# Block sums of the up projection's weights, added in DRAM during latent attention, with another order of its seven products and another loading of the latents' weights

## The chip, the cores and the metric

The kernel runs on one NeuronCore of a Trainium2 chip. The metric is device time in microseconds (us), as a median over executions. Engines: TensorE (PE) multiplies, VectorE (DVE), ScalarE (ACT) and GpSimd (POOL) work on elements, SyncE (SP) issues DMA transfers; POOL can issue them too.

## The reference

One encoder layer over two requests of 2048 and 256 tokens (D_MODEL 1024, eight heads of latent attention, eight of neighbourhood attention, D_FF 2816):

```python
h = rms_norm(x, g_mix_pre)
z = h @ w_in                                   # latents, rope key, nq, nk, nv
a = mla_attention(c_q, c_kv, k_rope, g_q_lat, w_q_up, g_kv_lat, w_kv_up)
n = neighborhood_attention(nq, nk, nv, na_rpb)
mix = jnp.concatenate([a, n], axis=-1) @ w_o
x = x + rms_norm(mix, g_mix_post)
h = rms_norm(x, g_ffn_pre)
x = x + rms_norm(conv_ffn(h, w_ffn_up, ffn_conv_w, ffn_conv_b, w_ffn_down), g_ffn_post)

def conv_ffn(x, w_up, conv_w, conv_b, w_down):
    h = x @ w_up                               # 1024 x 5632
    hp = jnp.pad(h, ((0, 0), (pad, pad), (0, 0)))
    hc = conv_b
    for t in range(CONV_W):                    # width 3, over positions
        hc = hc + hp[:, t:t + S] * conv_w[t]
    g, u = jnp.split(hc, 2, axis=-1)
    return (jax.nn.gelu(g, approximate=True) * u) @ w_down
```

All values are float32.

## The kernel before, in words

**Precision.** Each factor of a product is split into a high part (`split`: ACT copies it, L95) and a low part (DVE subtracts, L96), and three matmuls (`mm3`, L120 to L122) make one product.

**Order of work.** A tile scheduler puts the instructions of each engine in one order, which the engine then keeps; each DMA queue starts its transfers in the order in which its engine issues them. The stages: input projection (to some 280 us), neighbourhood attention (to some 700), preparation and loop of latent attention (794 to 1653), output projection in 18 tiles of 128 tokens (to some 1925), up projection (to some 2960), down projection.

**Neighbourhood attention** runs `n` = 144 iterations of half a unit, each with scores, softmax and transposes (`turn`: probabilities `pb` L404, their transposes `pT` L411, copies `pth`, `ptl`) and values. Between them `queries_rest` (in the first half) makes the remaining query and key projections, and `latents` (from iteration `mid + LATE` = 78) the latents' projection, a quarter of a token tile per call. At `mid` = 72 the latents' weights take the place of the weights `w2` of the first half: eight blocks are loaded through `qk_hl`, a pool of two buffers which also carries queries and keys to DRAM, and split into `w3h` and `w3l`.

**Latent attention** is a loop of 528 steps of 128 keys by 512 queries: scores `pS`, exponentials `ph` (ACT, L623, six buffers), low parts `pl` (DVE), a running sum `acc` (POOL, L634), and values some steps behind. `later` is a table from a step to what is done there.

**Up projection.** The product of weights (blocks W00, W01, W10, W11: gate or value rows by halves of D_MODEL) and inputs is made by seven products of block sums for each of three parts of the tokens (L1051) and 22 hidden tiles, 66 units. `PLAN` is the list of products; a product is 12 matmuls of 386 columns. Each needs a factor of weights (`w_factor`: a raw block or a block sum, 128x512, then split into `wh`, `wl`) and one of inputs (`x_factor`, once for each part, `xh`, `xl`; sums made by `x_source`, L1152). The results lie in PSUM in one of eight banks `pz`, two products add onto the bank of an earlier one (`onto`), and `s`, `v`, `t`, `hg`, `hu` are combinations of them (L1194 is the helper's line, on DVE or POOL); `conv` is the convolution (L1222 on ACT, L1225 on DVE), and POOL multiplies gate by value (L1241).

**Block sums of weights.** Five sums for each of 22 hidden tiles go to `ws_d` in DRAM. Those of hidden tiles 0 to 5 are made in the output projection (`weight_sums`, loads L138, additions on POOL L149, stores L144). Those of 6 to 21 are made in part 0 of the up projection (`w_source`: five additions on POOL, L1132, and five stores per hidden tile). Parts 1 and 2 load all of them from `ws_d`.

## Time and profile before

| | |
|---|---|
| median of three runs | 3509.68 us (3509.68, 3509.68, 3519.23) |
| the profiled execution | 3507.15 us, its span 3505.4 us |
| mean granted clock of TensorE | 0.989 |
| PE busy | 3368.9 us (96%) |
| DVE busy | 2385.9 us (68%) |
| ACT busy | 1837.8 us (52%) |
| POOL busy | 1376.2 us (39%) |

The span goes from the first to the last instruction of the profiled execution; its own time is some 2 us longer. A busy share is an average over stages that differ. The granted clock is TensorE's clock as a share of full speed, which is 2.4 GHz.

### The profile page before, as it was taken

How to read it: one execution, taken by the hardware profiler on the slowest of the kernel's cores; microseconds unless marked ns; L12 is line 12 of the kernel's file. 1: busy time of each engine (PE TensorE's matmuls, PEld its weight loads, DVE VectorE, ACT ScalarE, POOL GpSimd, SP SyncE). 2: the span in 40 equal slices, each digit the busy share in tenths (PEclk: the TensorE clock that was granted, in tenths of full speed). 3: DMA queues.
4: the chain of work that ended last, by engine and by line, in shares of the span. 5: the costliest groups of instructions: out<-in, count | busy, mean ns of one | idle time of the engine just before them, and what ended most of it. 6: DMA issues, size and time to landing. Idle time of an engine off the chain costs nothing.

```text
span 3505.4 us, 51290 instructions
## 1 busy us (share of the span) xinstructions
PE 3368.9 (96%) x17806; PEld 2913.6 (83%) x17806; DVE 2385.9 (68%) x3774; ACT 1837.8 (52%) x3463; POOL 1376.2 (39%) x1216
## 2 busy tenths in 40 slices
PE   8999989989999999999989999899999999999999
PEld 7889979967777777766778999899989999888887
DVE  5325555588988888898345999987789776224332
ACT  4225556567777777777234544555555554223121
POOL 0022323157777778775521477632232222000110
PEclk9999999999999999999999999999999999999999
DMA  8789889341000000011995655465546555434553
GB/s 269 253 258 231 213 191 237 122 149 26 13 15 14 16 14 13 18 47 48 267 256 150 195 170 172 144 192 149 149 113 194 151 150 179 149 117 134 187 186 125
DMA packets 338068, 497.24 MB, mean 142 GB/s; under 512 B 69584, under 2 KB 213072, under 8 KB 330832
## 3 DMA queue, kind: packets, MB, share of 16 engines
q1 hardware_dynamic: 302576, 417.87, 39.7%
q0 software_dynamic: 35232, 76.10, 8.6%
q8 instruction: 140, 2.29, 0.3%
q14 instruction: 120, 0.98, 0.1%
HBM read 337.90 MB, written 155.37 MB: 141 GB/s over the span
## 4 chain that ended last, share of the span: by engine, by line
PE 74%; DVE 10%; ACT 6%; DMA 5%; issue 3%; POOL 2%; SPq 1%; ACTq 0%; POOLq 0%; DVEq 0%
PE pz L1291 21%; PE po L122 6%; PE po L120 6%; PE po L121 6%; PE po L646 3%; PE pS L619 3%; PE pg L600 3%; PE pl L647 3%; PE pS L621 3%; PE pS L620 3%; PE pO L448 2%; DVE wl L96 2%; PE pT L120 2%; PE pT L411 2%; PE pT L122 1%
## 5 line engine op out<-in xcount | busy, mean ns | idle before, releaser
L1291 PE MATMUL pz<-xh,wh 128*128 128x386 f32 (+1 forms) x1848 | 633.3, 343 | 20.8 <-DVE hg L1194 11.5
L1291 PE MATMUL pz<-xl,wh 128*128 128x386 f32 (+1 forms) x1848 | 630.2, 341 | 6.1 <-DVE xl L96 5.7
L1291 PE MATMUL pz<-xh,wl 128*128 128x386 f32 (+1 forms) x1848 | 628.8, 341 | 6.0 <-DVE wl L96 6.0
L634 POOL TENSOR_TENSOR acc<-acc,ph 128x512 f32<-128x512 f32 x434 | 568.3, 1309 | 103.8 <-ACT ph L623 82.3
L96 DVE TENSOR_TENSOR wl<-raw,wh 128x512 fp32r<-128x512 f32 (+1 forms) x470 | 444.0, 953 | 36.2 <-ACT wh L95 36.0
L95 ACT CAST wh<-raw 128x512 fp32r<-128x512 f32 (+1 forms) x470 | 288.9, 627 | 235.4 <-PE pz L1291 221.3
L623 ACT ACTIVATE ph<-pS 128x512 fp32r<-128x512 f32 (+1 forms) x528 | 312.4, 592 | 183.5 <-PE pS L621 98.6
L626 DVE TENSOR_TENSOR pl<-pS,ph 128x512 fp32r<-128x512 f32 (+1 forms) x528 | 354.6, 673 | 71.9 <-ACT pS L624 68.3
L110 POOL TENSOR_TENSOR rs_r<-rs_m,mhalf 128x1 f32<-128x1 f32 (+1 forms) x90 | 74.3, 826 | 800.4 <-DVE rs_m L107 800.1
L1291 PEld LDWEIGHTS pz<-xh,wh 128*128 128x128 f32 x1848 | 350.5, 190 | 31.3 <-DVE hg L1194 16.6
L1291 PEld LDWEIGHTS pz<-xl,wh 128*128 128x128 f32 x1848 | 351.1, 190 | 8.1 <-DVE xl L96 7.3
L1291 PEld LDWEIGHTS pz<-xh,wl 128*128 128x128 f32 x1848 | 350.7, 190 | 7.5 <-DVE wl L96 7.4
L602 DVE TENSOR_REDUCE mx<-pg 128x1 f32<-128x512 f32 (+1 forms) x528 | 343.0, 671 | 12.6 <-PE pg L600 10.1
L1241 POOL TENSOR_TENSOR cg<-cg,cu 128x768 f32<-128x768 f32 (+1 forms) x66 | 165.2, 2503 | 445.3 <-DVE cu L1225 324.6
L122 PE MATMUL po<-dh,xr 128*128 128x512 f32 x792 | 311.7, 394 | 0.4 <-DVE xr L96 0.4
L121 PE MATMUL po<-dl,xr 128*128 128x512 f32 x792 | 311.8, 394 | 0.0
L120 PE MATMUL po<-dh,xr 128*128 128x512 f32 x792 | 311.6, 393 | 0.0
L624 ACT ACTIVATE pS<-pS 128x512 f32<-128x512 f32 (+1 forms) x528 | 311.5, 590 | 0.0
L96 DVE TENSOR_TENSOR xr<-xt,xr 128x1408 fp32r<-128x1408 f32 x37 | 60.6, 1639 | 330.8 <-ACT xr L95 330.8
L95 ACT CAST xr<-xt 128x1408 fp32r<-128x1408 f32 x37 | 50.7, 1369 | 382.1 <-PE po L121 368.3
L619 PE MATMUL pS<-ql,kbh 96*128 96x512 f32 (+1 forms) x528 | 215.2, 408 | 5.0 <-DVE pl L626 2.9
L621 PE MATMUL pS<-qh,kbh 97*128 97x512 f32 (+1 forms) x528 | 211.8, 401 | 0.1
(259 smaller groups left out, 7923.6 us busy)
## 6 DMA issues: line engine op xcount, KB each, us to landing
raw<-ws_d SPq DMA_DIRECT2D x250, 256.0 KB, 2.7
raw<-in_w_ffn_up_dram SPq DMA_DIRECT2D x164, 256.0 KB, 3.2
xt<-g_d SPq DMA_DIRECT2D x37, 704.0 KB, 4.4
graw<-g_d SPq DMA_DIRECT2D x35, 704.0 KB, 5.1
g_d<-cg SPq DMA_DIRECT2D x110, 192.0 KB, 2.3
ws_d<-raw SPq DMA_DIRECT2D x80, 256.0 KB, 2.0
xl<-xs_d POOLq DMA_DIRECT2D x18, 1024.0 KB, 8.8
xh<-xs_d POOLq DMA_DIRECT2D x18, 1024.0 KB, 7.1
```

Of the source, the lines that this page charges most:

```text
L95: self.nc.scalar.copy(out=hi, in_=src)
L96: self.nc.vector.tensor_tensor(out=lo, in0=src, in1=hi.bitcast(F32), op=ALU.subtract)
L120: mm(out=out, lhsT=lh, rhs=rh, start=start, stop=False)
L121: mm(out=out, lhsT=lh, rhs=rl, start=False, stop=False)
L122: mm(out=out, lhsT=ll, rhs=rh, start=False, stop=stop)
L602: nc.vector.tensor_reduce(out=u.mx[:, i, c:c + 1], in_=pg[:, :n], axis=AX.X, op=ALU.max)
L619: mm(out=pS[:, :nq], lhsT=u.kh[0:QKD, kc], rhs=u.ql[:, :nq], start=True, stop=False)
L621: mm(out=pS[:, :nq], lhsT=u.kh[:, kc], rhs=u.qh[:, :nq], start=False, stop=True)
L623: nc.scalar.activation(out=ph[:, :nq], in_=pS[:, :nq], func=AF.Exp, scale=scale)
L626: nc.vector.tensor_tensor(out=pl[:, :nq], in0=pS[:, :nq], in1=ph[:, :nq].bitcast(F32), op=ALU.subtract)
L634: eng.tensor_tensor(out=u.acc[:, :nq], in1=ph[:, :nq].bitcast(F32), op=ALU.add, in0=u.p0[:, :nq].bitcast(F32) if j == 1 else u.acc[:, :nq])
L1291: nc.tensor.matmul(out=pz[:, :w], lhsT=l[:, kk, :], rhs=r[:, kk, :w], start=onto is None and kk == 0 and e == 0, stop=kk == 3 and e == 2, ...
```

## The change

1. All block sums are made in DRAM, by transfers that POOL issues in the loop of latent attention: four sums instead of five, each in two halves of 11 hidden tiles (2.88 MB a transfer). Eight transfers copy a first block to `ws_d` (from step 20 on, one in eight steps), eight more add a second block or another sum to it (four from step 160, two from 270, two from 360). `weight_sums` in the output projection and `w_source` are gone.
2. The seven products use other sums and another order, (1, 5, 3, 7, 2, 6, 4); one product (4) adds onto another (7) instead of two. `value` comes before `gate`; one combination per unit moves from DVE to POOL (`hu`), another falls away.
3. The latents' weights come block by block: block k is loaded at iteration `mid - 12 + k` into a pool of its own, and split two iterations later into a slot of `w2`, which is now eight tiles. `latents` starts at `mid`.

```diff
-    def weight_sums(self, raw_buf, out_buf, todo):
...
+        block = lambda rc, js: a["w_ffn_up"].rearrange("(r j) p k c -> r j p (k c)", r=2)[
+            rc[0], js, :, 512 * rc[1]:512 * rc[1] + 512]
+        first, stages = [], [[], [], []]
+        def late(**k):
+            self.tc.keep_in_program_order(nc.gpsimd.dma_start(**k))
+        for i, (m, (b0, b1)) in enumerate(self.WSUM.items()):
+            for js in (slice(0, 11), slice(11, NFF)):
+                first.append(lambda i=i, b0=b0, js=js: late(out=self.ws_d[js, i], in_=block(b0, js)))
+                src = self.ws_d[js, list(self.WSUM).index(b1)] if isinstance(b1, int) else block(b1, js)
+                stages[max(0, i - 1)].append(lambda i=i, src=src, js=js: late(
+                    out=self.ws_d[js, i], in_=src, accum_op=ALU.add, max_dma_last_dim=2048))
+        return [first] + stages
...
+            w2 = [[w2p.tile([P, KD, P], F32R, name=f"w{2 * f + i}") for i in range(2)] for f in range(4)]
...
+            def load_lat(k):
+                raw = lwp.tile([P, LAT], F32, name="raw")
+                nc.sync.dma_start(out=raw, in_=a["w_in"][k * P:(k + 1) * P, 0:LAT])
+                def convert():
+                    wlat[k] = w2p.tile([P, 2, LAT], F32R, name=f"w{k}")
+                    self.split(raw, wlat[k][:, 0, :], wlat[k][:, 1, :])
+                return convert
...
+                if 0 <= i - (mid - 10) < KD:
+                    lat_w[i - (mid - 10)]()
+                if 0 <= i - (mid - 12) < KD:
+                    lat_w[i - (mid - 12)] = load_lat(i - (mid - 12))
+                if i == mid - 4:
+                    Rest.blocks = {0: fetch(0)}
                 if i == mid:
-                    wlat = [w[:, :, :LAT] for w in w_tiles(w2p, 3, 512)]
-                    Rest.n, Rest.blocks = 0, {0: fetch(0)}
-                    load_w(lambda: st.tile([P, 2, NB], F32, name="qk_hl").rearrange("p a b -> p (a b)"), wlat, 0, LAT)
-                if i >= mid + LATE and Rest.n < 4 * NT:
+                    Rest.n = 0
+                if i >= mid and Rest.n < 4 * NT:
                     latents()
...
+            for q, part in enumerate(self.weight_sums()):
+                for r, f in enumerate(part):
+                    later.setdefault((20, 160, 270, 360)[q] + 8 * r, []).append(f)
...
-            if t < 7:
-                sums()
-                sums()
-            if t == 7:
-                flush()
...
-    ORDER = (1, 5, 3, 4, 2, 7, 6)
-    WSUM = {1: ((0, 0), (1, 1), 1), 2: ((1, 0), (1, 1), 1), 5: ((0, 0), (0, 1), 1), 6: ((1, 0), (0, 0), -1),
-            7: ((0, 1), (1, 1), -1)}
-    WRAW = {3: (0, 0), 4: (1, 1)}
+    WSUM = {4: ((0, 1), (1, 1)), 5: ((0, 0), (0, 1)), 1: ((0, 0), 4), 2: ((1, 0), 1)}
+    WRAW = {3: (0, 0), 6: (1, 0), 7: (1, 1)}
...
-    PLAN = [(k, m) for k in range(3 * NFF) for m in (1, 5, 3, 4, 2, 7, 6)]
-    PLAN[4:9] = [(1, 1), (1, 5), (0, 2), (0, 7), (0, 6)]
-    NRAW = 13
+    PLAN = [(k, m) for k in range(3 * NFF) for m in (1, 5, 3, 7, 2, 6, 4)]
+    PLAN[4:9] = [(1, 1), (1, 5), (0, 2), (0, 6), (0, 4)]
+    NRAW = 10
...
-    def w_source(self, i):
...
+        def value(u):
+            tt(nc.vector, u.hu[:, 1, :u.w], u.b[6][:, :u.w], u.t[:, :u.w], 1)
+            u.cu = conv(u.hu, NFF + u.j, u.n, "u")
         def gate(u):
-            tt(nc.vector, u.hg[:, 0, :u.w], u.b[1][:, :u.w], u.v[:, :u.w], 1)
+            tt(nc.vector, u.hg[:, 0, :u.w], u.v[:, :u.w], u.b[7][:, :u.w], -1)
             u.cg = conv(u.hg, u.j, u.n, "g")
             nc.scalar.activation(out=u.cg[:, :, :u.n], in_=u.cg[:, :, :u.n], func=AF.Gelu_apprx_tanh)
+            nc.gpsimd.tensor_tensor(out=u.cg[:, :, :u.n], in0=u.cg[:, :, :u.n], in1=u.cu[:, :, :u.n], op=ALU.mult)
...
-            onto = {7: 1, 6: 3}.get(m)
+            onto = {4: 7}.get(m)
...
             if m == 2:
+                u.t = hp.tile([P, 388], F32, name="t")
+                tt(nc.vector, u.t[:, :w], u.v[:, :w], u.b[2][:, :w], -1)
                 u.hu = hp.tile([P, 2, 388], F32, name="hu")
-                tt(nc.vector, u.hu[:, 0, :w], u.b[2][:, :w], u.s[4][:, :w], 1)
-                u.t = hp.tile([P, 388], F32, name="t")
-                tt(nc.vector, u.t[:, :w], u.s[1][:, :w], u.b[2][:, :w], -1)
+                tt(nc.gpsimd, u.hu[:, 0, :w], u.s[7][:, :w], u.t[:, :w], -1)
```

The order of instructions moves at three places. The first is ACT at the middle of neighbourhood attention, before (`pb` are probabilities, `pth` and `o` copies of transposes and outputs, `w3h` the high parts of the latents' weights):

```order
L404 ACTIVATE pb_2358,den<-sS,mn 128x512
L95 CAST pth_2372<-pT 128x4x128
L95 CAST w3h<-qk_hl 128x416
L404 ACTIVATE pb_2360,den<-sS,mn 128x512
L451 COPY o<-pO 64x256
L95 CAST pth_2372<-pT 128x4x128
L95 CAST pth_2372<-pT 128x2x128
L404 ACTIVATE pb_2362,den<-sS,mn 128x256
L95 CAST pth_2366<-pT 128x4x128
L95 CAST w3h<-qk_hl 128x416
L451 COPY o<-pO 64x256
L95 CAST w3h<-qk_hl 128x416
```

And after, some iterations ahead of the middle:

```order
L95 CAST pth_2413<-pT 128x4x128
L95 CAST pth_2413<-pT 128x2x128
L95 CAST w_5038<-raw 128x416
L95 CAST w_5093<-raw 128x416
L391 ACTIVATE pb_2403,den<-sS,mn 128x576
L95 CAST pth_2407<-pT 128x4x128
L438 COPY o<-pO 64x256
L391 ACTIVATE pb_2405,den<-sS,mn 128x576
L180 ACTIVATE qk_hl<-pT 128x256
L95 CAST pth_2407<-pT 128x4x128
L95 CAST pth_2407<-pT 128x2x128
```

The conversions of the latents' weights read `raw` instead of `qk_hl`, and stand two by two among the rows of one iteration. The second place is POOL in the loop of latent attention, after; before, it holds the same rows `acc` (L634 there) and `s` without the transfer:

```order
L670 TENSOR_TENSOR s<-s,o 64x512
L636 TENSOR_TENSOR acc<-acc,ph 128x512 x2
L135 DMA ws_d<-in_w_ffn_up_dram 11x128x512
L636 TENSOR_TENSOR acc<-acc,ph 128x512 x4
L636 TENSOR_TENSOR acc<-ph 128x512
L636 TENSOR_TENSOR acc<-acc,ph 128x512 x5
```

A transfer of 11x128x512 elements is issued between two additions. The third is POOL in part 0 of the up projection, before (`raw` are the sums of weights):

```order
L1194 TENSOR_TENSOR v<-s_21917,s_21875 128x386
L1132 TENSOR_TENSOR raw<-raw 128x512 x5
L1241 TENSOR_TENSOR cg<-cg,cu 128x2x384
L1194 TENSOR_TENSOR v<-s_22076,s_22034 128x386
L1132 TENSOR_TENSOR raw<-raw 128x512 x5
L1241 TENSOR_TENSOR cg<-cg,cu 128x2x384
```

And after:

```order
L1161 TENSOR_TENSOR hu<-s_21863,t 128x386
L1161 TENSOR_TENSOR v<-s_21958,s_21979 128x386
L1208 TENSOR_TENSOR cg<-cg,cu 128x2x384
L1161 TENSOR_TENSOR hu<-s_22023,t 128x386
L1161 TENSOR_TENSOR v<-s_22118,s_22139 128x386
L1208 TENSOR_TENSOR cg<-cg,cu 128x2x384
```

The five additions per hidden tile are gone, and `hu` is a row of its own between two multiplications.

## Rows read from the trace of the kernel before

**Rows 1.** The page's first part, all of it: busy us, share, instructions.
```profile
PE 3368.9 (96%) x17806; PEld 2913.6 (83%) x17806; DVE 2385.9 (68%) x3774; ACT 1837.8 (52%) x3463; POOL 1376.2 (39%) x1216
```
**Rows 2.** Stretches by windows: busy us (instructions) by engine, granted clock, DMA.
```profile
core 0: us, PE busy (x) PEld busy (x) DVE busy (x) ACT busy (x) POOL busy (x), PEclk, DMA share, GB/s
480.00:520.00 40.00, 26.86 (x150) 24.74 (x151) 20.04 (x46) 21.09 (x51) 7.87 (x13) 0.79 0.92 181
520.00:680.00 160.00, 159.80 (x1102) 153.74 (x1101) 93.10 (x224) 100.54 (x237) 40.09 (x56) 1.00 0.73 189
800.00:1500.00 700.00, 690.73 (x3096) 497.45 (x3095) 623.17 (x1092) 542.88 (x1059) 554.84 (x433) 1.00 0.06 15
1665.00:1820.00 155.00, 138.30 (x655) 113.51 (x654) 66.12 (x92) 44.51 (x70) 68.64 (x90) 0.96 0.94 268
2000.00:2260.00 260.00, 246.71 (x1357) 238.64 (x1355) 258.99 (x261) 125.93 (x212) 187.03 (x107) 1.00 0.54 171
2260.00:2300.00 40.00, 28.59 (x129) 27.03 (x129) 39.00 (x33) 19.72 (x26) 20.52 (x7) 0.83 0.50 158
2300.00:2600.00 300.00, 300.00 (x1695) 300.00 (x1694) 232.28 (x329) 168.15 (x268) 69.43 (x41) 1.00 0.55 154
2600.00:2640.00 40.00, 32.53 (x162) 31.09 (x161) 39.59 (x34) 20.92 (x29) 17.42 (x6) 0.91 0.31 98
```
**Rows 3.** Timeline near 487 and 508: start, us, engine, line, [idle before].
```profile
486.69 0.54 ACT L95 CAST w3h<-qk_hl 128x416 fp32r<-128x416 f32 x1 [9.56 <-DMA qk_hl<-in_w_in_dram]
...
507.60 0.54 ACT L95 CAST w3h<-qk_hl 128x416 fp32r<-128x416 f32 x1 [4.23 <-DMA qk_hl<-in_w_in_dram]
```
**Rows 4.** PE's waits over the whole span: us in total, times, longest us.
```profile
PE pt L948 <- DMA at<-att_d: 15.5, 4, 7.1
...
PE pT L411 <- ACT pb L404: 10.0, 1, 10.0
```
**Rows 5.** Timeline of SP in the output projection: a store in each tile.
```profile
1686.28 0.52 SPq L990 DMA_DIRECT2D x_d<-x  x1
...
1823.69 0.52 SPq L990 DMA_DIRECT2D x_d<-x  x1
...
1912.31 0.52 SPq L990 DMA_DIRECT2D x_d<-x  x1
```
**Rows 6.** DMA view: transfers by issue, count, KB each, median us to landing.
```profile
ws_d<-xr SPq DMA_DIRECT2D x12, 640.0 KB, 5.6
...
xr<-in_w_ffn_up_dram SPq DMA_DIRECT2D x48, 128.0 KB, 4.8
```
**Rows 7.** Groups of instructions in part 0, 2000 to 2250.
```profile
L96 DVE TENSOR_TENSOR wl<-raw,wh 128x512 fp32r<-128x512 f32 x111 | 140.7, 1279 | 0.0
...
L1132 POOL TENSOR_TENSOR raw<-raw 128x512 f32<-128x512 f32 x74 | 125.4, 1694 | 63.2 <-DVE wl L96 61.0
```
**Rows 8.** The same in part 1, 2310 to 2590.
```profile
L96 DVE TENSOR_TENSOR wl<-raw,wh 128x512 fp32r<-128x512 f32 x135 | 101.1, 750 | 18.4 <-ACT wh L95 18.4
...
L1241 POOL TENSOR_TENSOR cg<-cg,cu 128x768 f32<-128x768 f32 x19 | 41.9, 2207 | 180.3 <-DVE cu L1225 161.7 <-ACT wh L95 9.4 <-ACT s L1231 9.3
...
L1194 POOL TENSOR_TENSOR v<-s,s 128x386 f32<-128x386 f32 x19 | 20.8, 1095 | 37.1 <-ACT s L1231 35.0 <-DMA g_d<-cg 2.1
...
L1194 DVE TENSOR_TENSOR hu<-pz,s 128x386 f32<-128x386 f32 x19 | 10.6, 559 | 17.5 <-PE pz L1291 17.5
```
**Rows 9.** Timeline of the second changeover.
```profile
2601.11 6.47 DVE L96 TENSOR_TENSOR wl<-raw,wh 128x512 fp32r<-128x512 f32 x3
...
2602.42 4.01 POOL L1152 TENSOR_TENSOR xt<-xr,xr 128x1552 f32<-128x1552 f32 x1
```
**Rows 10.** POOL's issues of line L225: ns min/median/max, first and last start.
```profile
L225 POOL DMA_DIRECT2D v<-nav_d x24: 759/878/1117, 107.1 to 614.3; - x24
```
**Rows 11.** ACT's line L623, one for each step of latent attention.
```profile
L623 ACT ACTIVATE ph<-pS x528: 375/598/622, 794.0 to 1653.3; 128x512 fp32r<-128x512 f32 x168, 128x256 fp32r<-128x256 f32 x8
```
**Rows 12.** ACT's waits, 794 to 1653: us in total, times, longest.
```profile
ACT ph L623 <- POOL acc L634: 5.8, 5, 1.2
```

More of the change, by code (lines that the diff above doesn't have):

```diff
@@ L475, in queries_rest @@
                     Rest.pq = ps_t.tile([P, 512], F32, name="pT")[:, :NB]
-                qk_products(w2, f, Rest.pq, range(4 * half, 4 * half + 4), *Rest.blocks[b])
+                qk_products(w2[f], Rest.pq, range(4 * half, 4 * half + 4), *Rest.blocks[b])
                 if half == 1:
@@ L990, in tail @@
             nc.sync.dma_start(out=self.x2_d[:, :, c0:c0 + P], in_=x2)
-        room = [self.ff_xr.tile([P, 4, 784], F32, name=f"xr{i}").rearrange("p a b -> p (a b)") for i in range(2)]
-        place = [0, 0]
-        def buf(i, n, size):
-            place[i] = (place[i] + 1) % n
-            return room[i][:, place[i] * size:(place[i] + 1) * size]
-        sums, flush = self.weight_sums(lambda: buf(0, 6, 512), lambda: buf(1, 2, 1280),
-                                       [(j, c) for j in range(self.NSUM) for c in range(2)])
         nxt = head(0)
@@ L1108, in load_w @@
         j = k % NFF
-        if self.NSUM <= k < NFF:
-            for rc in {1: [(0, 0), (1, 1)], 5: [(0, 1)], 3: [(1, 0)]}.get(m, []):
-                t = self.blocks[k, rc] = self.ff_raw.tile([P, 4, P], F32, name="raw")
-                nc.sync.dma_start(out=t, in_=a["w_ffn_up"][j + rc[0] * NFF][:, 4 * rc[1]:4 * rc[1] + 4, :])
-            return
         t = self.raws[i] = self.ff_raw.tile([P, 4, P], F32, name="raw")
@@ L1295, in ffn @@
                 self.x_factor(p + 1, m)
[L1296 removed]
+            if m in (1, 5, 7):
                 keep(u, m)
```

112 lines of the change are left out of this document (33 added, 79 removed).

## The prediction, made blind

> **What bounds the kernel now.** I began with the busy times of the whole span. TensorE (PE) is busy for 3368.9 of 3505.4 us [rows 1]: nothing that another engine does counts unless PE stops for it, and all that PE ever loses is 136 us of standing still plus what it loses in speed while busy. So the question for each edit is where PE falls behind its own pace now. For that I cut the span into stretches and compared, in each, the number of matmuls with that of a clean stretch of the same stage [rows 2]; the reader should look at the count and at PEclk, since a matmul counted as busy may be running slowly. Four places fall short, and the edits touch all four:
>
> - The middle of neighbourhood attention, 480 to 520: 150 matmuls in 40 us at a clock of 0.79, where the clean stretch 520 to 680 does 1102/160 = 6.89 per us. 40 x 6.89 = 276, so 126 are missing: 18 us.
> - The output projection, 1665 to 1820, with the DMA engines busy 0.94 of the time. Its stores give the tile's period: from 1823.69 to 1912.31 seven periods of 12.66 us, from 1686.28 to 1823.69 nine that take 137.41 instead of 113.9 [rows 5]. That is 23.5 us.
> - Part 0 of the up projection, 2000 to 2260: VectorE (DVE) is busy 258.99 of 260 us, and PE does 1357 matmuls where part 1's pace, 1695/300 = 5.65 per us, gives 1469: 112 missing, 20 us.
> - The two changeovers between parts: 129 instead of 226 in 2260 to 2300 (17 us), 162 instead of 226 in 2600 to 2640 (11 us).
>
> Elsewhere PE is close to its pace: 300 of 300 us in part 1, 690.73 of 700 in latent attention.
>
> **A. Latents' weights block by block.** Now, at the middle iteration, eight blocks are loaded and converted through the same two buffers that pass the queries to DRAM, and the conversions stand in ACT's and DVE's order among those of the attention. The trace shows what that does: the conversion of one block waits 9.56 us for its load, and PE waits 10.0 us for the probabilities that stand behind it on ACT; a second load holds ACT for 4.2 us more [rows 3, 4]. The clock then falls, and matmuls run at the lower level of 1.2 GHz for a while (0.79 is the mean of both). The new code loads each block two iterations (some 6 us) before it is converted, into buffers of its own, and splits the weights that lie there before into eight tiles, so that each slot comes free by itself. Of the 18 us I count 14 as gone; 4 stay for the loads of the next head's keys and tables, which crowd the same place (DMA busy 0.92 [rows 2]). Bounds: 10 (only the one wait goes) and 20 (all of it, and the bit of clock after 520).
>
> **B. No weight sums in the output projection.** 48 loads of 128 KB and 12 stores of 640 KB leave SP's queue there [rows 6]: 6.3 + 7.9 = 14 MB, 53 us of DMA at the 268 GB/s of [rows 2]. PE's longest wait in this stage is for the attention tile's load (15.5 us in four waits [rows 4]). The loss has two halves. The periods before 1775 lose 13 us, and there the sums' transfers lie in the queue; these go. The later 10 us come at the two loads of the normalized input (3 MB) and the up projection's first weights, with the sums already done; the change leaves the 3 MB, and takes away some weight loads. I count half of these: 13 + 5 = **18** with bounds of 8 (the first half only in part, since each tile still moves some 2 MB) and 23.5.
>
> **C. Part 0 of the up projection.** What slows DVE there is GpSimd's (POOL's) additions. The same subtraction of DVE, 128x512, takes 1279 ns in part 0 and 750 ns in part 1; the additions L1132 (1694 ns, five for each hidden tile from 6 on) are what part 1 hasn't got [rows 7, 8]. The change drops them, with their stores. In their place POOL gets one more 128x386 subtraction per hidden tile, at 1095 ns by the row of its sister v; DVE loses one of its five (559 ns by [rows 8]). So part 0 should look like part 1, and PE get back **20 us** (bounds 15 and 20). All parts then carry POOL 69.43/300 + 1.1/14.9 = 31% of the time, DVE some 77% (232.28/300 now): PE is still the slowest. The new subtraction reads t, which DVE has just made, and DVE's next product of the unit reads it in turn: DVE, POOL, DVE, 0.55 + 1.1 us, with one product of PE (12 matmuls, 2.1 us at that pace) between. It is hidden while POOL isn't in its 2207 ns multiplication; if it is, DVE stands for up to 2.2 us while it has 14.9 x 0.23 = 3.4 us of slack per unit (84 matmuls at 5.65 per us are 14.9 us). A bank of PSUM is now used again after 9.3 products, 20 us, instead of 11; what holds a bank, POOL's v and DVE's hg among it, takes 1.1 and 0.56 us [rows 8], far below that.
>
> **D. Changeovers.** The weights' subtractions swell there (three in 6.47 us instead of 2.25) while POOL adds one 4.01 us block of the input's sums [rows 9]. The change keeps three such sums on POOL, but part 0's POOL has no backlog any more at the first changeover. I take 6 us off the first, nothing off the second; bounds 14 less and 8 more (the input's sums come in another order, and one 4 us sum lands in front of a product that needs it, twice).
>
> **E. Sixteen transfers in latent attention.** The new DRAM sums are issued by POOL between its additions acc. Nothing here shows an accumulating DMA. The nearest rows: POOL's issue of a load with 512 to 1024 rows takes 759 to 1117 ns, median 878 [rows 10]; a transfer here has 1408 rows, so I estimate 1.3 us, and twice that, as an upper estimate, for one that adds: 8 x 1.3 + 8 x 2.6 = 31 us of POOL over 560 us. POOL is busy 554.84 of 700 us there, so it has a fifth of its time to spare, and six buffers ph let it fall some 6 us behind before ACT must wait (today 5.8 us in all [rows 12]). The bound below is 0, the one above 15 (half of it uncovered). I take **4**, nearer to 0 since two issues are eight steps, 13 us, apart and each is below the 6 us.
>
> **F.** The latents now start and end six iterations earlier, so the attention's last six run without that filler. A latents step is six matmuls, 0.9 us at 6.89 per us; six of them could cost 5 us, and 0 if PE has other work; I take **2**.
>
> **Sum**, against the profiled execution's 3507.15 us: -14 - 18 - 20 - 6 + 4 + 2 = -52, which gives 3455. The median of the runs lies 2.5 us above the profiled one, so **3458**; the rivals' times below are medians too. A measurement can tell about 0.3% (10.5 us) from no change.
>
> **Rivals.**
> - *Slower: the sums don't get done in time.* From step 270 on an issue on POOL first waits for an accumulation of the round before; acc stands in order behind it, and once POOL is more than some 6 us late ph runs out and PE loses the rest. The last of these waits, at step 368, is (368 - 160) x 1.63 us (528 steps in 859 us [rows 11]) = 339 us after the accumulations begin and needs six of them: 6 x 2.88 MB, read twice, is 34.6 MB, so 102 GB/s are wanted, where the output projection shows 268 and latent attention itself uses 15 [rows 2]. It decides at 34.6 MB/(339 + 6 + 52) us = 87 GB/s: below that POOL's waits cost more than the 52 us gained. At 75 GB/s they cost 116 us: 3574. Against it: a factor of three to the shown rate. For it: nothing here shows a transfer from DRAM to DRAM or one that adds. 6 in 100.
> - *The sums are cheap but POOL gives nothing back in the up projection.* With the new subtraction DVE waits for POOL in every hidden tile, 66 times 0.4 us, which eats the 26 us of C and D: 3485. For it: POOL and DVE stretch each other [rows 7 to 9]. Against it: DVE's slack. 12 in 100.
> - *The output projection stays bound by its transfers*, or the middle gap returns through the loads of head 4: B gives 8 and A 8: 3474. 15 in 100.
> - *Issues starve.* DVE is busy 623.17 of 700 us in latent attention. If POOL writes descriptors only while DVE rests, an issue of 1.3 us takes 1.3/0.11 = 12 us, of which ph covers 6: 16 x 6 = 96 us on PE instead of E's 4, so 3550, slower. It decides at some 9 us an issue (16 x 3 = 52). Against it: the issues of [rows 10] lie in a stage where DVE is busy 93.10 of 160 us [rows 2], which by the same reckoning makes 0.88 us out of 0.37, and the longest is 1.1 us. 3 in 100. The Trainium skill ("SBUF — State Buffer", section "SBUF: two separate sides") says that a DMA issued by GpSimd is starved while VectorE runs an operation that locks their shared port. By the page's own figures, 620 ns becoming some 3100, an issue would take 6.5 us as an estimate, and ph would cover most of it; no run here shows it so far.
>
> The forecast itself has 0.57, with a range of its own of 3440 to 3472. The second and third rival, 0.12 and 0.15, are faster too: 0.84. Several mishaps together that end within 10.5 us of now have 0.07, and the two slower rivals 0.09. The range goes down to 3438, where A, B and D are at their better ends, and up past the second rival's 3485 to 3495.
>
> The Trainium skill ("Collectives: The Full Stack", section "The bandwidth ceiling: the fold count and why AG ≠ RS ≠ AR") says that a transfer which adds needs two source reads and so runs at half the rate of a copy. By that, as an estimate, the six would take 17.3 MB at 134 GB/s, 129 us of the 339; no run here shows it so far.
>
> **What would show it.** Right: 480 to 520 with some 230 matmuls or more and no 10 us wait for pb; an even period of 12.7 us in the output projection; the 128x512 subtraction at some 750 ns in part 0 and DVE at some 77%; sixteen POOL issues of 1 to 3 us in latent attention with no wait for ph. Wrong: POOL waiting on a DMA near steps 270 and 360 with ACT's ph waiting for acc; issues of 5 us and more; DVE waiting for hu in every hidden tile; a period above 13.5 us in the output projection.

## The result, and the profile after

The changed kernel takes **3563.75 us** (median of four runs, 3562.18 to 3565.88), before 3509.68: a ratio of 1.0153, 95% interval 1.0127 to 1.0180. It is slower by 54 us where 52 less were forecast, and it lies outside the range.

I compared the two traces by the places where one stage hands over to the next: the first and last `ph` of latent attention, the first product of the up projection. In us, from before to after:

| part of the span | before | after | |
|---|---|---|---|
| all ahead of the first `ph` | 794.0 | 786.4 | -7.6 |
| loop of latent attention, first to last `ph` | 859.3 | 942.6 | **+83.3** |
| last `ph` to the first product of the up projection | 257.1 | 254.1 | -3.0 |
| up projection, first to last of its `xh`, `wh` products | 1034.7 | 1015.3 | -19.4 |
| the rest | | | +2.1 |
| span | 3505.4 | 3560.9 | +55.5 |

So of the gains that I had counted those ahead of the loop and in the up projection are there by half or more, that of the output projection hardly, and one stage loses more than all of them. The page of the changed kernel, its PE row and the clock (answering to [rows 1]):

```profile
PE 3407.2 (96%) x17806; PEld 2928.6 (82%) x17806; DVE 2340.0 (66%) x3724; ACT 1852.3 (52%) x3479; POOL 1295.5 (36%) x1158
...
PEclk9999999998898999999899999999999999999999
```

PE has the same 17806 instructions and is busy 38 us longer. More busy time with the same work is a matter of speed, or of what "busy" hides; the clock's four eights stand between 801 and 1780 us (slices of 89 us), in the loop and just behind it. Its windows (columns as in [rows 2]), and under them the same loop in the trace of before:

```profile
480.00:520.00 40.00, 38.22 (x256) 35.87 (x257) 24.30 (x61) 24.97 (x61) 11.51 (x20) 1.00 1.05 257
786.40:1729.00 942.60, 893.19 (x3734) 620.35 (x3734) 775.70 (x1323) 667.32 (x1292) 679.80 (x528) 0.95 0.28 67
860.00:960.00 100.00, 89.95 (x323) 57.25 (x322) 71.24 (x117) 56.70 (x108) 63.20 (x51) 0.86 0.44 162
1060.00:1160.00 100.00, 91.26 (x359) 60.46 (x359) 75.90 (x127) 62.91 (x124) 70.05 (x54) 0.90 0.68 117
2060.00:2320.00 260.00, 257.27 (x1453) 256.95 (x1451) 207.37 (x259) 145.38 (x226) 84.84 (x54) 1.00 0.50 149
2320.00:2360.00 40.00, 36.02 (x190) 35.14 (x191) 39.38 (x38) 22.47 (x34) 17.83 (x8) 0.96 0.52 166
```
```profile
794.00:1653.30 859.30, 841.02 (x3738) 602.36 (x3738) 766.21 (x1330) 666.02 (x1293) 661.18 (x514) 1.00 0.08 20
```

The loop's 83.3 us come apart here: PE stands 49.4 us (942.60 - 893.19) instead of 18.3, which is 31 us, and the same matmuls, four fewer of 3738, are busy for 52 us longer at a mean clock of 0.95. From 860 to 960 PE does 323 matmuls, where [rows 2] gives 3096/700 = 4.42 per us, 442.

The first suspects were the new transfers. POOL's issues of them, and ACT's steps with what ACT waited for:

```profile
L135 POOL DMA_DIRECT2D ws_d<-in_w_ffn_up_dram x12: 1079/1098/1951, 814.0 to 1137.1; - x12
...
L135 POOL DMA_DIRECT2D ws_d<-ws_d x4: 1898/1914/1933, 1284.9 to 1460.4; - x4
```
```profile
L625 ACT ACTIVATE ph<-pS x528: 375/597/619, 786.4 to 1729.0; 128x512 fp32r<-128x512 f32 x168, 128x256 fp32r<-128x256 f32 x8
...
  POOL acc L636: 5.6, 7
```
```profile
ACT ah L95 <- POOL acc L636: 10.7, 5, 3.1
```

The eight copies and four of the additions read the weights, four additions add sums to sums. An issue takes 1.1 us (copies) or 1.9 us (additions), 24 us of POOL's time in all; no row shows POOL waiting for a DMA. For its steps ACT waits 5.6 us for `acc`, as before [rows 12]. POOL's lateness shows at another place: ACT waits 10.7 us to convert finished sums (`ah`, the high part of `acc`), where before it waited for POOL not at all, and PE's wait for what comes of them (`al`, the low part, made by DVE) is 4.4 us instead of 2.2. All additions have been issued by 1460 and landed 39 us later at most, long before the first use. Neither of the two slower rivals took place. PE's waits in the loop name mostly VectorE instead:

```profile
PE pS L621 <- DVE pl L628: 14.0, 22, 1.8
PE pg L602 <- DVE mx L604: 8.8, 31, 0.7
PE pg L602 <- ACT qh L95: 7.4, 4, 2.9
```

`pg` is the guard product of a later head (L602, L600 before): scores of which DVE takes row maxima (`mx`). Before, PE waited for `mx` twice, for 0.9 us, for `pl` nine times, for 2.9, and its list has no wait for `qh`, a later head's queries. What is new is seen in the order of PE's instructions, around one such place (before above, after below; `po`, `pl` are the value products):

```
L619 MATMUL pS<-ql,kbh_7801 128x512
L620 MATMUL pS<-qh,kbl_7802 128x512
L621 MATMUL pS<-qh,kbh_7801 128x512
L600 MATMUL pg<-kbh_7803,qh 128x512
L647 MATMUL pl<-pl,vt_7799 65x512
L619 MATMUL pS<-ql,kbh_7801 128x512
```
```
L648 MATMUL po<-ph,vt_7847 128x512
L602 MATMUL pg<-kbh_7851,qh 128x512
L649 MATMUL pl<-pl,vt_7847 65x512
L602 MATMUL pg<-kbh_7851,qh 128x512 x11
L648 MATMUL po<-ph,vt_7847 128x512 x2
L621 MATMUL pS<-ql,kbh_7849 128x512
```

Before, guards stand by ones and twos among the steps. After, ten rows of four and more hold 96 of them. Of the 3152 score, guard and value matmuls of the loop only 2013 stand in stretches (of 12 or more) that both orders share. On the chip such a place looks like this (timeline of after):

```profile
840.99 0.49 PE L602 MATMUL pg<-kbh,qh 96*128 96x512 f32 x1 [0.19 <-DVE mx L604]
841.44 3.28 DVE L604 TENSOR_REDUCE mx<-pg 128x1 f32<-128x512 f32 x5
...
843.50 1.09 PE L602 MATMUL pg<-kbh,qh 96*128 96x512 f32 x2 [0.23 <-DVE mx L604]
...
844.78 0.50 PE L602 MATMUL pg<-kbh,qh 96*128 96x512 f32 x1 [0.19 <-DVE mx L604]
...
845.97 2.84 PE L602 MATMUL pg<-kbh,qh 96*128 96x512 f32 x4
...
847.90 1.27 POOL L636 TENSOR_TENSOR acc<-ph 128x512 f32<-128x512 f32 x1 [8.00 <-ACT ph L625]
```

Five maxima take DVE 3.28 us, 0.66 each, and PE's guards come at that pace (four in 2.84 us, counted as busy). No scores are made meanwhile, so ACT has no `pS`, and POOL's addition waits 8.00 us for `ph`: the whole chain of the steps stands while DVE reduces.

My theory from here on (**order**): the scheduler, given sixteen more instructions on POOL, put TensorE's instructions of the loop into a worse order. The rival (**transfers**): their bytes, issues or descriptors slow the loop, and the order makes little difference. In the expectations they are theory O and theory T.

### The profile page after: what moved, and what is told of

The parts are those of the page before. It is cut to its first block, busy times and chain, and to the rows that moved or that the text cites. A ratio compares the mean times of both kernels' runs of the same rounds, so it can differ in the third digit from the quotient of the medians.

```text
span 3560.9 us, 51128 instructions
## 1 busy us (share of the span) xinstructions
PE 3407.2 (96%) x17806; PEld 2928.6 (82%) x17806; DVE 2340.0 (66%) x3724; ACT 1852.3 (52%) x3479; POOL 1295.5 (36%) x1158
## 4 chain that ended last, share of the span: by engine, by line
PE 51%; DVE 6%; ACT 2%; issue 1%; DMA 1%; POOL 1%; SPq 0%; POOLq 0%; ACTq 0%; DVEq 0%
PE pz L1258 23%; PE po L120 7%; PE po L122 7%; PE po L121 7%; DVE wl L96 2%; PE po L648 1%; PE pS L621 1%; PE pg L602 1%; PE pl L649 1%; PE pS L623 1%; PE pS L622 1%; ACT ph L625 1%; DVE xl L96 1%; DVE mx L604 1%; DVE cg L1192 1%
## 5 line engine op out<-in xcount | busy, mean ns | idle before, releaser
L1161 POOL TENSOR_TENSOR v<-s,s 128x386 f32<-128x386 f32 (+1 forms) x66 | 102.6, 1554 | 433.6 <-DVE cg L1192 300.3
L95 ACT CAST xr<-xt 128x1408 fp32r<-128x1408 f32 x37 | 50.6, 1368 | 385.0 <-PE po L121 369.5
L602 PE MATMUL pg<-kbh,qh 96*128 96x512 f32 (+1 forms) x528 | 219.4, 433 | 20.1 <-DVE mx L604 8.8
L621 PE MATMUL pS<-ql,kbh 96*128 96x512 f32 (+1 forms) x528 | 222.9, 422 | 15.7 <-DVE pl L628 14.0
## 6 DMA issues: line engine op xcount, KB each, us to landing
ws_d<-in_w_ffn_up_dram POOLq DMA_DIRECT2D x12, 2816.0 KB, 14.3
```

Of the source, the lines that this page charges most:

```text
L95: self.nc.scalar.copy(out=hi, in_=src)
L621: mm(out=pS[:, :nq], lhsT=u.kh[0:QKD, kc], rhs=u.ql[:, :nq], start=True, stop=False)
```

## The experiments

Each group of kernels was timed beside the kernel before, whose median lay between 3502.6 and 3505.6. "Loop" is first to last `ph`.

| run | loop us | median us | ratio to before (95%) |
|---|---|---|---|
| e1 | 1092.6 | 3743.47 | 1.0689 (1.0668 to 1.0711) |
| e2 | 1141.0 | 3788.50 | 1.0818 (1.0791 to 1.0845) |
| e3 | 1089.9 | 3702.99 | 1.0572 (1.0557 to 1.0588) |
| e4 | 1087.2 | 3693.61 | 1.0549 (1.0531 to 1.0567) |
| e5 | 926.4 | 3541.94 | 1.0117 (1.0100 to 1.0135) |
| e6 | 873.5 | 3489.59 | 0.9962 (0.9950 to 0.9973) |
| e7 | 874.3 | 3485.65 | 0.9947 (0.9928 to 0.9967) |
| e8 | 882.8 | 3505.54 | 1.0004 (0.9993 to 1.0015) |
| e9 | 859.5 | 3479.23 | 0.9927 (0.9898 to 0.9956) |
| e10 | 873.4 | 3488.88 | 0.9955 (0.9940 to 0.9971) |
| e11 | 872.0 | 3479.58 | 0.9932 (0.9909 to 0.9955) |
| e12 | 860.8 | 3492.87 | 0.9963 (0.9952 to 0.9975) |
| e13 | 879.5 | 3497.41 | 0.9987 (0.9972 to 1.0002) |
| e14 | 963.6 | 3576.10 | 1.0204 (1.0174 to 1.0235) |
| e15 | 862.3 | 3479.66 | 0.9929 (0.9911 to 0.9947) |
| e16 | 863.4 | 3468.38 | 0.9891 (0.9871 to 0.9912) |
| e17 | 903.4 | 3521.36 | 1.0055 (1.0040 to 1.0071) |

### One order for both kernels: e1, e2, e3

e1 is the kernel before, e3 the changed one, both with TensorE's matmuls and transposes of the loop held in the order in which the program writes them:

```diff
+            pe = nc.tensor
+            plain = pe.matmul, pe.transpose
+            pe.matmul = lambda *p, **k: tc.keep_in_program_order(plain[0](*p, **k))
+            pe.transpose = lambda *p, **k: tc.keep_in_program_order(plain[1](*p, **k))
             i = 0
```

> The kernel before, with TensorE's instructions in the loop of latent attention kept in the order in which the program writes them (scores, one or two guard products, values). It is the base for the next two. The loop of before took 859 us (first to last ph). Both theories: the loop stays within 2% of that, 845 to 875 us, and the time within 3500 to 3525 us.

> The kernel after, with all its transfers, and TensorE's instructions in the loop kept in the order in which the program writes them. Theory O: the loop falls from 943 to 855 to 875 us and the time to 3475 to 3495. Theory T: the loop stays above 920 us and the time above 3540.

Without a transfer in it, e1's loop takes 1092.6 us: the order alone is worth 233 us, far more than I expected of it. With all sixteen transfers, as the change writes them, e3 takes 1089.9. By the letter e3 meets theory T's forecast (above 920) and not theory O's; but both were built on a loop of some 860 us for e1, which had missed, and only beside e1 does e3 speak: in a common order the transfers cost nothing. (A loop with PE standing 173 us could hide what a dense one doesn't; e15 and the trace of after answer that below.)

e2 is e1 with 12 of the 16 guards of three heads written in one row:

```diff
-                    spread(side, u.guards(), first + 1, end)
+                    g = u.guards()
+                    if u.nkt == 16 and u.h in (0, 1, 4):
+                        spread(side, g[:4], first + 1, first + 5)
+                        side[end].extend(g[4:])
+                    else:
+                        spread(side, g, first + 1, end)
```

> As e1, and in the heads 0, 1 and 4 the guard products of a unit (row maxima of the scores) stand as four and then twelve in a row instead of one or two per step, as they stand after the change; no transfers are added. Theory O (the order of TensorE's instructions costs the 83 us): twelve guards take VectorE 12 x 0.67 = 8.1 us and TensorE only 2.9 us, so TensorE stands some 5 us in each of 11 bunches and the clock falls behind them; the loop takes 910 to 945 us, the time 3560 to 3595. Theory T (the transfers and their issues cost it): the loop as in e1, at most 875 us, the time at most 3525.

The loops of e1 and of e2 by windows:

```profile
792.30:1884.90 1092.60, 919.71 (x3746) 649.96 (x3745) 787.06 (x1334) 683.76 (x1292) 651.81 (x515) 0.92 0.06 16
```
```profile
786.10:1927.10 1141.00, 964.80 (x3745) 663.79 (x3745) 794.08 (x1334) 683.24 (x1292) 653.23 (x515) 0.89 0.06 15
```

Counted from e1's loop and not from 860 us, as the forecast did, theory O holds: eleven rows cost 48.4 us, 4.4 each, where some 5 were expected. PE stands only 3 us longer; 45 are busy time, at a clock of 0.89 instead of 0.92.

### The scheduler's order, with the transfers written in other ways: e5, e6, e8, e13, e14, e17

e5 holds only the guards in the order of the program; all else is the scheduler's.

```diff
-                    nc.tensor.matmul(out=pg[:, :n], lhsT=u.qh[0:QKD, i * P:(i + 1) * P],
-                                     rhs=u.kh[0:QKD, k0:k0 + n], start=True, stop=True)
+                    tc.keep_in_program_order(nc.tensor.matmul(out=pg[:, :n], lhsT=u.qh[0:QKD, i * P:(i + 1) * P],
+                                                              rhs=u.kh[0:QKD, k0:k0 + n], start=True, stop=True))
```

> The kernel after, with its transfers as they are, and only the guard products kept behind what TensorE has to do before them in the program, so that they can't gather ahead of a unit's scores: none stand more than four in a row, where after the change 96 of 504 stand in ten rows of up to thirteen. The rest of the order may still differ from before. Theory O (the order costs the 83 us): the loop falls from 943 to 865 to 900 us, the time to 3485 to 3520. Theory T (the transfers cost it): the loop stays above 925.

A miss: 16 us of 83 come back, and 926.4 us even lies on the side of theory T, by 1.4. The rows of guards aren't the whole cause; 2161 matmuls stand as before instead of 2013, and the rest of the order is still the other one. PE's list in e5 names other work:

```profile
PE pl L653 <- DVE al L96: 11.5, 10, 3.1
...
PE pm L120 <- DVE kbl L96: 7.6, 6, 1.4
```

`kbl` are the low parts of a later head's keys. Before, the wait for `al` was 2.2 us, and there was none for `kbl`. At e2's price of 4.4 us for twelve, the 96 guards of after come to an estimated 35 us, less than half of the 83.

e6 writes the same transfers with rows first and hidden tiles second, and one in 16 steps instead of one in eight:

```diff
+            for w in ("out", "in_"):
+                k[w] = k[w].rearrange("j p k -> p j k")
             self.tc.keep_in_program_order(nc.gpsimd.dma_start(**k))
...
-                    later.setdefault((20, 160, 270, 360)[q] + 8 * r, []).append(f)
+                    later.setdefault((20, 160, 270, 360)[q] + 16 * r, []).append(f)
```

> The kernel after, the same sixteen transfers of the same bytes, but each written with its 128 rows as the first dimension instead of the 11 hidden tiles, and sixteen steps apart instead of eight. The scheduler then gives TensorE nearly the order of before in the loop (2977 of 3152 matmuls lie in stretches of twelve or more that stand in both). Theory O: the loop takes 858 to 870 us and the time is 3478 to 3495. Theory T: the bytes and the issues are the same, so the loop stays above 925 us and the time above 3545.

The same bytes in as many transfers, and the loop falls to 873.5, 3.5 us above theory O's range and far from theory T's; 2977 of 3152 matmuls now stand as before. e13 and e14 take the two edits apart: rows first at eight steps, and tiles first, as the change has them, at 16.

```diff
-                    later.setdefault((20, 160, 270, 360)[q] + 16 * r, []).append(f)
+                    later.setdefault((20, 160, 270, 360)[q] + 8 * r, []).append(f)
```

> As e6, but eight steps apart as in the change: the shape alone. TensorE's order is in between: guard products stand five in a row at most, but only 2187 of 3152 matmuls lie in stretches that stand in the order of before too. If the order costs the time, the loop lies between e6 and after, 875 to 905 us. If the spacing costs it, it is above 925. If the shape of the transfers costs it, it is as e6, at most 878.

> The kernel after with its transfers as they are, sixteen steps apart instead of eight: the spacing alone. TensorE's order is of the kind of after (96 guard products in twelve rows of four to thirteen, 1306 of 3152 matmuls in stretches of before). If the order costs the time, the loop takes 930 to 960 us. If the spacing costs it, it takes at most 890.

More room between the transfers makes the tiles-first kernel worse (963.6, with 1306 matmuls as before), so the room isn't what helps. Rows first helps at either spacing (879.5, 873.5). e13's 879.5 is within the range for the order and only 1.5 us above that for the shape, so it doesn't decide between the two. Is it the shape itself, or the order that comes with it? e17 keeps rows first and makes eight transfers of all 22 tiles out of sixteen:

```diff
-            for js in (slice(0, 11), slice(11, NFF)):
+            for js in (slice(0, NFF),):
```

> As e6, but one transfer for all 22 hidden tiles of a sum: eight issues instead of sixteen, the same bytes, rows first as in e6. The scheduler gives TensorE an order far from before: 1438 of 3152 matmuls in common stretches, 39 guard products in five rows of up to ten. If the order costs the time, the loop takes 890 to 940 us. If it is the tile-first shape that costs it (or the number of issues), the loop takes 860 to 876 us, as e6.

Rows first, half as many issues, and the loop is back at 903.4, with 1438 matmuls as before and 39 guards in rows of four and more. So the shape isn't what decides it. e8 sends single tiles, 176 transfers of 256 KB, each by itself tiles first:

```diff
-            for js in (slice(0, 11), slice(11, NFF)):
+            for js in [slice(q, q + 1) for q in range(NFF)]:
...
-                    later.setdefault((20, 160, 270, 360)[q] + 8 * r, []).append(f)
+                    later.setdefault((20, 160, 270, 360)[q] + r * (1, 2, 3, 3)[q], []).append(f)
```

> The kernel after, each sum made tile by tile: 88 copies and 88 additions of 256 KB instead of 16 of 2.88 MB, the same bytes, one to three steps apart. TensorE's order in the loop is that of before in 3129 of 3152 matmuls. POOL issues 176 times; at 0.6 to 1.0 us each that is 105 to 175 us more for it, where it is idle some 170 of 859. Theory O: the loop takes 860 to 900 us, all over 860 by what POOL is late. Theory T (the bytes cost it): above 925 us.

3129 matmuls stand as before, and the loop takes 882.8. Here POOL's time is seen: 132 issues of a median 526 ns and 44 of 806, 119 us in all, and ACT waits 16.6 us for the sums `ah<-acc` (after: 10.7).

Set in a row, the loop follows the order only roughly: with 3129, 2977, 2187, 2161, 2013, 1438 and 1306 matmuls as before it takes 882.8, 873.5, 879.5, 926.4, 942.6, 903.4 and 963.6 us. The count is a rough measure: e13 and e5 have nearly the same, 47 us apart, and e17 is faster than e5 and after with fewer, because it takes any score, guard or value product for any other of its kind. Counted in the traces with the n-th product of a kind the same as the n-th alone, they are 3116, 2964, 2618, 2106, 2110, 2395 and 1731 in the same sequence. By this count the loop gets longer as fewer stand as before, except for e8, where POOL's issues add to it, and for e5 and after, which have nearly the same count 16 us apart. The orders of ACT, DVE and POOL move along with TensorE's, and which engine's order costs what isn't shown.

### What the transfers cost when the order is kept: e9, e15

e9 is e6 with sixteen issues of one tile each. It leaves most of the sums out and puts a raw block in their place, so its time tells of issues and order alone.

```diff
-            for js in (slice(0, 11), slice(11, NFF)):
+            for js in (slice(0, 1), slice(11, 12)):
...
-            nc.sync.dma_start(out=flat, in_=self.ws_d[j, list(self.WSUM).index(m)])
+            nc.sync.dma_start(out=t, in_=a["w_ffn_up"][j][:, 0:4, :])
```

> As e6, but each of the sixteen transfers moves one hidden tile instead of eleven, and the up projection loads a raw block in place of each block sum, so that part of the computation is left out; TensorE's order in the loop is that of before in 3129 of 3152 matmuls. e6's loop took 873.5 us against 859.3 before the change. If the transfers' bytes and the length of their issue cost these 14 us, the loop takes 857 to 863 us here. If the rest of the change costs them (what stands in front of the loop, the memory that its buffers share), it takes 870 us or more.

e15 does all the work: rows first, 32 transfers of five or six tiles.

```diff
-            for js in (slice(0, 11), slice(11, NFF)):
+            for js in (slice(0, 6), slice(6, 11), slice(11, 17), slice(17, NFF)):
...
-                    later.setdefault((20, 160, 270, 360)[q] + 16 * r, []).append(f)
+                    later.setdefault((20, 160, 270, 360)[q] + (8, 6, 10, 10)[q] * r, []).append(f)
```

> As e6, but 32 transfers of five or six hidden tiles, six to ten steps apart: the same bytes, and TensorE's order is that of before in 3113 of 3152 matmuls (e6: 2977). If the rest of the order costs the 14 us that e6 still loses to before, the loop takes 859 to 865 us. If the transfers and their issues do, it takes 870 to 880, since 32 issues hold POOL a little longer than sixteen.

e15's loop by windows:

```profile
779.30:1641.60 862.30, 840.21 (x3734) 600.88 (x3734) 767.05 (x1323) 665.73 (x1292) 694.08 (x544) 1.00 0.31 73
```

e9 takes 859.5 and e15 862.3, with 3129 and 3113 matmuls as before. By its own two branches e9 would speak for the bytes and issues as the cost of e6's 14 us, but its order had also come back to that of before; e15, with all the bytes in that order, tells that it was the order. All the bytes, and twice the issues, cost some **3 us**, and PE's row is that of before: 840.21 busy, clock 1.00. So the rival is refuted in a dense loop as well, for transfers with rows first.

For the transfers as the change writes them, the trace of after has both kinds of steps. The first transfers of each group start while TensorE still has its order of before. 24 steps have such an order and a transfer under way: 19 to 25 (a copy), 160 to 164 (an addition of weights), 269 to 275 and 360 to 364 (additions of sums). They take 36.8 us in all, in before 36.9. The longest two of these stretches, and the steps 26 to 84 behind the first, where the order is the other one (windows of after):

```profile
811.80:824.00 12.20, 12.03 (x53) 8.81 (x53) 12.03 (x21) 8.92 (x19) 9.70 (x8) 1.00 0.53 193
1282.90:1295.60 12.70, 12.66 (x55) 9.34 (x54) 12.32 (x21) 8.01 (x16) 12.14 (x10) 1.00 0.48 82
824.00:961.50 137.50, 123.91 (x446) 78.70 (x445) 100.83 (x168) 75.72 (x147) 83.19 (x67) 0.86 0.45 164
```

PE does 4.3 matmuls per us in the first two, near the 4.42 of before, and 3.2 in the third, which takes 137.5 us instead of 95.4. So, as far as these 24 steps reach, the transfers alone don't slow a dense loop. The other half is less clean: of the 190 steps in which the order differs, the 127 with a transfer under way lose 86.8 us, and the 63 without one lose none (-2.6). That the other order alone costs time is shown by e2, and in e14 and e17 by some 7 and 9 us in such steps; that it would cost all of the 83 us with no transfer beside it isn't shown.

### The other parts one by one: e4, e7, e10, e11, e12

After the change the output projection's tiles come more evenly, but the first stores its result 50.4 us after the last `ph`, before 33.0. SP's queue in after:

```profile
1740.08 6.44 SPq L935 DMA_DIRECT2D x_d<-zc  x3
1746.56 0.67 SPq L942 DMA_DIRECT2D na<-natt_d  x1
...
1779.38 0.52 SPq L995 DMA_DIRECT2D x_d<-x  x1
...
1985.04 0.52 SPq L995 DMA_DIRECT2D x_d<-x  x1
```

Three stores of zeros hold the queue for 6.44 us, with the first tile's load of `natt_d` behind them. e4 (on e3) and e7 (on e6) move them to the third tile:

```diff
-        zc = sm.tile([P, KD, 2], F32, name="zc", bufs=1)
...
+            if t == 2:
+                zc = sm.tile([P, KD, 2], F32, name="zc", bufs=1)
+                nc.gpsimd.memset(zc, 0.0)
+                for c0, n in ((0, 1), (SP + 1, 2), (XC - 1, 1)):
+                    tc.keep_in_program_order(nc.sync.dma_start(out=self.x2_d[:, :, c0:c0 + n], in_=zc[:, :, :n]))
```

> As e3, and the zeros for the padding columns are set and stored in the third tile of the output projection instead of ahead of the first, where their stores stand in SP's queue before the first tile's loads. The first tile's store came 33 us after the last ph before the change and 50 us after it. Theory H (the first tile waits for the loads behind those stores): the 50 us fall to 33 to 42 and the time is 8 to 17 us below e3. Rival: the up projection's weight loads, which now stand there, or the last additions of latent attention are what it waits for; then it gains less than 4 us.

> As e6, with the zeros of the padding columns stored in the third tile of the output projection as in e4, which gained 9 us there. Theory O and H: 3468 to 3487, 6 to 12 us below e6, and below both kernels. Theory T: above 3535.

The first store comes 42.1 us after the last `ph` in e4 (e3: 50.6) and 43.8 in e7 (e6: 48.5). The medians fall by 9.4 and 3.9 us. The second, for which 6 to 12 were expected, is too little to be told from nothing; the first can be told. e10 also holds back the up projection's first eight weight loads, with `tc.keep_in_program_order` around both loads of `load_w`:

```diff
-            self.load_w(i)
+            self.load_w(i, self.tc.keep_in_program_order)
```

> As e7, and the first eight weight loads of the up projection keep their place in the program, in the ninth tile of the output projection, instead of standing among the first tiles' loads in SP's queue. In e7 the first tile's store comes 44 us after the last ph, before the change 33. If those loads delay the first tiles, the 44 us fall to 35 to 40 and the time is 4 to 9 us below e7. If the first tile waits for its natt block, whose load now stands behind the last store of latent attention, it gains less than 3 us.

The first store comes at 41.4, and the time doesn't fall (3488.88). What is left of the late start, some 8 us, stays open: the first tile's load of `natt_d` also stands behind the last store of `att_d` now, where before it stood ahead; another order there wasn't tried.

e11 is e7 with the new subtraction back on DVE, and so tests the second rival:

```diff
-                tt(nc.gpsimd, u.hu[:, 0, :w], u.s[7][:, :w], u.t[:, :w], -1)
+                tt(nc.vector, u.hu[:, 0, :w], u.s[7][:, :w], u.t[:, :w], -1)
```

> As e7, with the combination hu on VectorE instead of POOL. Second rival of the prediction (VectorE waits for POOL's hu in every hidden tile): the up projection, 1014 us in e7 from its first to its last hi-hi product, becomes 10 to 30 us shorter. Forecast's view (TensorE sets the pace inside the parts): it stays within 5 us, and the time within 0.3% of e7.

The up projection takes 1011.2 us instead of 1014.0. Some 3 us, not the rival's 26.

e12 is the kernel before with part 3 of the change alone, all its hunks in neighbourhood attention; the core of them:

```diff
+                if 0 <= i - (mid - 10) < KD:
+                    lat_w[i - (mid - 10)]()
+                if 0 <= i - (mid - 12) < KD:
+                    lat_w[i - (mid - 12)] = load_lat(i - (mid - 12))
...
-                    load_w(lambda: st.tile([P, 2, NB], F32, name="qk_hl").rearrange("p a b -> p (a b)"), wlat, 0, LAT)
...
-                if i >= mid + LATE and Rest.n < 4 * NT:
+                if i >= mid and Rest.n < 4 * NT:
```

> The kernel before with the third part of the change alone: the latents' weights block by block. TensorE's order in the loop of latent attention is that of before to the last matmul. The prediction's terms A and F: 12 us faster (5 to 18), 3485 to 3500 against some 3503; the stretch of 40 us at the middle does 230 matmuls or more instead of 150. Rival: the loads that move ahead cost as much in the front of the attention, and the time is within 4 us of before.

11.6 us faster; TensorE's order in latent attention is that of before, and the gap is gone (window of e12):

```profile
480.00:520.00 40.00, 40.00 (x277) 38.53 (x276) 23.54 (x58) 25.58 (x61) 10.29 (x17) 1.00 0.95 220
```

### The best of the parts: e16

e16 is e15 with the edits of e7 and e11.

> e15 with the handover of e7 and hu on VectorE as in e11. If the pieces add up, the time is 3470 to 3482 us, at or a little below e11's 3480, and below both kernels.

3468.38 us: faster than before by 1.1% and than the change by 95 us. In its profiled span, against before: ahead of the first `ph` -10.6, loop +4.1, output projection -10.2, up projection -21.3, rest +3.2. Its PE row:

```profile
PE 3356.6 (97%) x17806; PEld 2911.4 (84%) x17806; DVE 2351.7 (68%) x3790; ACT 1850.3 (53%) x3479; POOL 1219.6 (35%) x1108
```

## Why the prediction was wrong

**E failed.** The step counted POOL's issues (31 us at most, 0 to 15 of it on the path) and asked whether `ph` would cover them. That was right as far as it went: 24 us of issues, ACT's wait for `acc` in its steps unchanged, and 3 us against my 4 where the order is kept (e15); the 10.7 us that ACT waits at `ah` I hadn't looked for. What the step left out is that the sixteen instructions, held in their place, are an input to the scheduler, which orders all engines. I looked at the new rows on POOL, and never laid TensorE's order in the loop beside the old one. It would have shown rows of up to 13 guards, and `mx` on DVE as the work in front of each. The missing term is some 80 us: 83.3 where the step has 4. That the order carries it is shown by e3 (same transfers, common order, no cost), by e6, e13 and e17 (same bytes, other orders, 873.5 to 903.4), by e15, and by the 24 steps of after with a transfer under way and the order of before, which lose nothing. Which part of the order costs how much is only partly shown: e2 prices a row of twelve at 4.4 us where nothing else moves, but e5 got only 16 us by taking the rows away. Why the scheduler chooses so differently for such small edits stays open.

**A**: right. 256 matmuls in 480 to 520 instead of 150, 15 us of the 18, and e12 gives 11.6 us for A and F together (-14 + 2 = -12). In the full change the first part of the span keeps only 7.6.

**B**: right for the tiles' periods, wrong in its sum, since it put the start of the first tile at nothing. Sixteen periods take 1985.04 - 1779.38 = 205.66 us, 12.85 each; [rows 5] has 226.03: -20.4, where I said -18. But the first tile's store comes 17.4 us later behind the last `ph` (50.4 instead of 33.0), which I didn't look for, and of my -18 only -3.0 is left.

**C and D**: of -26 came -19.4. Part 0 runs at full pace at last (1453 matmuls in 260 us, 1469 wanted), and the first changeover does 190 of 226 instead of 129, the second 193 instead of 162 [rows 2]. But the stretches behind them do less than before, 1659 and 1669 matmuls in 300 us each instead of 1695 and 1698, which takes back 65 matmuls, 11.5 us (window behind the first changeover of after):

```profile
2360.00:2660.00 300.00, 294.15 (x1659) 293.51 (x1658) 244.77 (x304) 166.96 (x262) 104.52 (x62) 1.00 0.51 153
```

DVE's subtraction didn't fall to part 1's 750 ns, and POOL's new row takes 1329 ns instead of the 1095 that I took (groups in part 0 of after):

```profile
L96 DVE TENSOR_TENSOR wl<-raw,wh 128x512 fp32r<-128x512 f32 x121 | 111.3, 922 | 1.9 <-ACT wh L95 0.3
...
L1161 POOL TENSOR_TENSOR hu<-s,t 128x386 f32<-128x386 f32 x17 | 22.6, 1329 | 49.3 <-DVE t L1161 49.3
```

The new row isn't what holds the subtraction up: over the same 260 us of part 0 it takes 921 ns in e7 and 914 in e11, which has `hu` on DVE. The reason stays open. It did no harm in part 0, since DVE's 207.37 of 260 us leave room.

**F**: not seen apart from A.

**The rivals.** The sums were done in time, and no issue starved, so both slower rivals were wrong though the time was slower: each priced the transfers. The Trainium skill's rule on the shared port ("SBUF — State Buffer", section "SBUF: two separate sides") didn't show: issues took 1.08 to 1.95 us in a loop of which DVE was busy 82% (775.70 of 942.60 us). There the Trainium skill speaks of operations that lock the port; whether DVE's operations in this loop do, no run shows. The Trainium skill's rule on adding transfers ("Collectives: The Full Stack", section "The bandwidth ceiling: the fold count and why AG ≠ RS ≠ AR"), given there for the reduce step of a collective, agrees in size with this trace (DMA view of after, median us to landing last):

```profile
ws_d<-in_w_ffn_up_dram POOLq DMA_DIRECT2D x12, 2816.0 KB, 14.3
...
ws_d<-ws_d POOLq DMA_DIRECT2D x4, 2816.0 KB, 27.3
```

The first row holds eight copies and four additions, the second additions alone, whose median is twice as long. But in the packets of the trace a copy is 704 of 4096 bytes and an addition, written with `max_dma_last_dim=2048`, 1408 of 2048, so that the second read is the reason isn't shown. 2.88 MB in 27.3 us are 106 GB/s, or 211 counted with both reads as the first rival counts, above the 87 at which it decides. The third rival was half true (-3.0), through the late first tile and not through transfers.

## What to carry to other kernels

Where a scheduler orders the instructions, an edit on one engine is also an edit of the order on all others: lay the order of the engine that bounds the kernel, before and after, side by side through every stage that the edit touches, and price each row of instructions that has become longer by the slowest engine that it feeds (here this gives an estimated 35 of the 83 us: a sign, and not the sum). When a stage gets slower and the new instructions in it show no waits, look for the same instructions in another order. Test it by holding both kernels to one order, and try other ways of writing the same transfers, since here those alone moved the loop between 862 and 964 us.

## What the runs showed of the hardware

- An addition in DRAM, as written here, cost its issuer more: POOL took 1.9 us to issue one (1408 packets of 2048 bytes) and 1.1 us for a copy of as many bytes (704 packets of 4096), and additions of sums to sums landed in 27.3 us, the rest, mostly copies, in 14.3. With rows first it was 19.0 and 12.8 us (e6). How much of this is the adding and how much the smaller packets wasn't tried.
- PE can be counted as busy for 90% and still be slow: from 860 to 960 it did 323 matmuls at a granted clock of 0.86, where 442 are the pace of before. Guards that come at the pace of DVE's maxima count as busy (four in 2.84 us). Of the 83 us, 52 are in busy time, not in idle time.
